# Input projection weights in 384-column half-row chunks, first convolution tap on ScalarE, channel transposes one tile later

## The chip, the core and the metric

The kernel runs on one core of one Trainium2 chip. The metric is device time in microseconds (us) of one execution; the time before is the median of three runs, 3180.53 us. TensorE (PE) loads weights (PEld) and multiplies; VectorE (DVE), ScalarE (ACT) and GpSimd (POOL) do the elementwise work; SyncE (SP) issues nearly all DMAs from one queue. Each engine runs its own instructions strictly in the order in which they were built.

## What is computed

One encoder layer over 2048 tokens of width 1024, all in float32. The part that the change touches is the first stage and the two branches that feed on it:

```python
h = rms_norm(x, g_mix[i])
proj = h @ w_in[i]                       # 1024 -> 2304 columns
q, k, v = proj[..., :512], proj[..., 512:640], proj[..., 640:768]
u = proj[..., 768:]                      # 1536 channels
ya = attention_group(q, k, v, ...)       # 8 query heads, 2 key heads
up = jnp.pad(u, ((0, 0), (1, 1), (0, 0)))
uc = conv_b + sum(up[:, j:j + L] * conv_w[j] for j in range(3))
v, x1, x2 = jnp.split(uc, 3, axis=-1)
z = x2 * long_conv(x1 * long_conv(v, H[0]), H[1])     # by FFT, filters from a small network
```

After it come the output projection, a mixture of experts, an embedding gate and a final norm, which the change leaves as they are.

## The kernel before

The projection is `stage_in` (line 105). It works on four quarters of 512 tokens. For each it loads four tiles of 128 tokens, normalises them, transposes them (L176) and splits them in a high and a low float32r part (`xh`, `xl`), since every float32 product is made of three float32r ones (`product`, L146 to 151). The weights are loaded (L134, `raw`) and split the same way in `split_w`: ACT rounds the high part (L139), and POOL (L89) or DVE (L143) subtracts it to get the low part.

Columns 0 to 767 (q, k, v) go through `tokens` (L182): three chunks of 256 columns, four token tiles each, with tokens as the stationary side, so each matmul streams 256 columns; ACT copies the result into a tile `stg`, which is stored to DRAM once per chunk (L190). Columns 768 on go through `channels` (L193): twelve tiles of 128 channels per quarter, channels on partitions and 512 tokens streamed. ACT copies the product into `U` (L205). The three-tap convolution is three DVE instructions: L210 multiplies the middle tap and adds the bias, L213 runs twice for the other two taps. PE then transposes the result back to tokens (L220), and ACT or DVE copies it into `stg` (L224, L226), which goes to DRAM (`uc_d`).

The whole runs beside a second stream. `interleave` (L92) builds two generators together, by the costs that they yield: the left one is `stage_in` and then attention, the right one is `stage_filter` (it generates the long filters: `gen`, a first FFT step L448 to L450, a second one L295), then `stage_hyena` (the long convolutions), then three tiles of the embedding projection (L1522 to L1540, `Ple`). The framework's scheduler then fixes the order on each engine. In `stage_hyena` every step keeps its result in one PSUM tile `ph`, of which there is only one: `step1` (L505) is the first FFT step, `mid` is a spread over frequencies (L295), a product on DVE (L529) and a gather (L308), and `back` (L545) is the inverse step. Between steps the data goes through DRAM. There are 32 of each. Attention runs in 16 units; their score matmuls are L806 and L809, the value ones L819, and `pa` (L741) are row maxima for later units. From the ninth unit on attention's PSUM banks include the two that hyena and `Ple` leave.

Of the kernel before, what the change touches and what calls it, by code (L numbers as in the profile page):

```python
# [8 lines left out]
F32 = mybir.dt.float32  # L9
F32R = mybir.dt.float32r  # L10
# [3 lines left out]
AF = mybir.ActivationFunctionType  # L14
ALU = mybir.AluOpType
# [3 lines left out]
P = 128  # L19
S = 2048  # L20
D = 1024
# [12 lines left out]
HY_LEAD = 0  # L34
HB = 3
FI_LATE = 1.5
GB = 8
GHB = 1
RB, WB = 13, 8
# [65 lines left out]
def stage_in(K, st, x, g_mix, w_in, conv_w, conv_b, qkv_d, uc_d, pa, attn):  # L105
# [16 lines left out]
    K.uc_done, K.banks_free = 0, False  # L122

    def consts():
        crow = pc.tile([48, P], F32, name="crow")
# [6 lines left out]
    def load_w(c0, n, pool, tag):  # L132
        raw = pool.tile([P, 8, n], F32, tag=tag, name="raw")
        nc.sync.dma_start(raw, w_in[:, c0:c0 + n].rearrange("(k p) n -> p k n", p=P))  # L134
        return raw

    def split_w(raw, n, pool, tags, on_pool, bufs=2):
        wh, wl = [pool.tile([P, 8, n], F32R, tag=tag, name=nm, bufs=bufs) for tag, nm in zip(tags, ("wh", "wl"))]
        nc.scalar.copy(wh, raw)  # L139
        if on_pool:  # L140
            K.lo_pool(wl, raw, wh)
        else:
            nc.vector.tensor_tensor(out=wl, in0=raw, in1=wh.bitcast(F32), op=ALU.subtract)  # L143
        return wh, wl

    def product(ps, left, right):  # L146
        for k in range(8):
            (lh, ll), (rh, rl) = left(k), right(k)
            nc.tensor.matmul(ps, lh, rh, start=(k == 0), stop=False)  # L149
            nc.tensor.matmul(ps, lh, rl, start=False, stop=False)  # L150
            nc.tensor.matmul(ps, ll, rh, start=False, stop=(k == 7))  # L151

    for h in range(NQ):
        last, first = h == NQ - 1, h > 0
        xh, xl = [[pa.tile([P, 4, HT], F32R, tag=f"{nm}{q}", name=nm) for q in range(2)] for nm in ("xh", "xl")]
        cols = [2, 0, 1] if last else [0, 1, 2]
        raws = []
        for t in range(HTT):
            r0 = h * HT + t * P
            xt = px.tile([P, D], F32, tag="xt", name="xt")  # L160
            nc.sync.dma_start(xt, x[r0:r0 + P])
            if r0 == 0:
                nc.sync.dma_start(gB, rows_bcast(g_mix))
            if t < 2:
                raws.append(load_w(cols[t] * 256, 256, praw, "raw"))
# [16 lines left out]
        def tokens(c, wh, wl):  # L182

            stg = pa.tile([P, HTT, 256], F32, tag="stg", name="stg", bufs=2)
# [8 lines left out]
        def channels(ct, stg, wh, wl):  # L193
# [10 lines left out]
            product(ps, lambda k: (wh(k), wl(k)), lambda k: xs(k, slice(None)))  # L204
            nc.scalar.copy(U[:, o0:o0 + HT], ps)  # L205
            if not last:
                nc.gpsimd.tensor_copy(bnd[:, ct], U[:, o0 + HT - 2:o0 + HT])
            n_out = HT + o0 - 1
            acc = pa.tile([P, HT + 4], F32, tag="acc", name="acc", bufs=2)
            nc.vector.tensor_scalar(out=acc[:, :n_out], in0=U[:, 1:1 + n_out], scalar1=wcol(1),  # L210
                                    scalar2=wcol(3), op0=ALU.mult, op1=ALU.add)
            for j in (0, 2):
                nc.vector.scalar_tensor_tensor(out=acc[:, :n_out], in0=U[:, j:j + n_out], scalar=wcol(j),  # L213
                                               in1=acc[:, :n_out], op0=ALU.mult, op1=ALU.add)
            if first:
                nc.gpsimd.tensor_copy(fix[:, h - 1, ct:ct + 1], acc[:, 0:1])
            pt = pst.tile([P, 512], F32, tag="pt", name="pt")
            for k in range(HTT):
                t0 = o0 - 1 + k * P
                nc.tensor.transpose(pt[:, k * P:(k + 1) * P], acc[:, t0:t0 + P], K.ident)  # L220
            dst = stg[:, :, ct % 2 * P:(ct % 2 + 1) * P]
            src = pt.rearrange("p (k c) -> p k c", k=HTT)
            if ct % 2:
                nc.scalar.copy(dst, src)  # L224
            else:
                nc.vector.tensor_copy(dst, src)  # L226

        for c in cols:
            raw = raws.pop(0) if raws else load_w(c * 256, 256, praw, "raw")
            if h == 0 and c == 0:  # L230
                consts()
            yield from tokens(c, *split_w(raw, 256, pw, ("wh", "wl"), not (c == 2 or (h == 0 and c < 2))))
        if last:
            while not K.filter_done:
                yield 0.05
            s_e.close()
            pb = attn.open(lambda tag: pst.tile([P, 512], F32, tag="pt", name=tag))
            ahead = attn.begin()
            raws = [load_w(768 + i * P, P, pb, "raw") for i in range(2)]
        for ct in range(12):  # L240
            part, cs = ct // 4, slice(ct // 2 % 2 * 256, (ct // 2 % 2 + 1) * 256)
            if last:
                raw = raws.pop(0)
                w4 = split_w(raw, P, pb, ("w", "w"), ct % 3 != 2, 4)
                if ct < 10:
                    raws.append(load_w(768 + (ct + 2) * P, P, pb, "raw"))
                wh, wl = [lambda k, w=w: w[:, k] for w in w4]
            else:
                if ct % 2 == 0:
                    raw = load_w(768 + ct * P, 256, praw, "raw")  # L250
                    w4 = split_w(raw, 256, pw, ("wh", "wl"), ct % 6 != 4)
                wh, wl = [lambda k, w=w: w[:, k, ct % 2 * P:(ct % 2 + 1) * P] for w in w4]
            if ct % 2 == 0:
                stg = pa.tile([P, HTT, 256], F32, tag="stg", name="stg", bufs=2)
            channels(ct, stg, wh, wl)
            yield 5.6
            if last:
                for _ in range(2):
                    if next(ahead, "end") != "end":
                        yield 0.44  # L260
# [1534 lines left out]
def block_kernel(tc, A, out):  # L1795
    K = Kit(tc)
    nc = tc.nc
# [9 lines left out]
    with ExitStack() as st:  # L1807
# [97 lines left out]
```

## Time and profile before

| | |
|---|---|
| median of three runs (lowest, highest) | 3180.53 us (3178.24, 3187.92) |
| the profiled execution, its span | 3189.39 us, 3187.4 us |
| PE busy | 2893.6 us, 91% |
| DVE, ACT, POOL busy | 66%, 43%, 37% |
| DMA, mean over the span | 197 GB/s |

Busy shares are means over stages with different limits; a stage is read by cutting it out of the span. "PEclk" is the TensorE clock that was granted in a stretch, as a share of 2.4 GHz; at 0.5 the engine runs at 1.2 GHz. A stretch loses time on PE in two ways: PE stands idle, or it works at the low clock.

### The profile page before, as it was taken

What the parts mean: (1) busy time and instruction counts of PE and PEld (TensorE: products, weight loads), DVE (VectorE), ACT (ScalarE), POOL (GpSimd) and SP (SyncE); (2) the same over time, 40 slices, a digit from 0 to 9 for tenths busy, and PEclk for the clock granted to TensorE, in tenths of its full rate; (3) what the DMA queues carried; (4) which work ended last, traced back from release to release, by engine and by line L of the source; (5) the groups of instructions that cost most, each with busy time, mean ns of one, the idle gap of its engine ahead of it and who ended that gap; (6) DMA issues with size and microseconds to landing.
All of it is one profiled execution on the core that took longest, in us unless ns stands there. A gap on an engine that the chain in (4) does not pass through costs nothing. (4 is left out here: it accounts for less than half of the span.)

```text
span 3187.4 us, 50724 instructions
## 1 busy us (share of the span) xinstructions
PE 2893.6 (91%) x19065; PEld 1942.2 (61%) x19065; DVE 2088.4 (66%) x2770; ACT 1357.0 (43%) x2040; POOL 1186.7 (37%) x1090
## 2 busy tenths in 40 slices
PE   7989898878899999759999999989999999998887
PEld 5767686655444453424444388866667777775766
DVE  5877767455687566527787644366667777775665
ACT  3343343432343334225444432245556666664332
POOL 1434544341365455228887543001111211221443
PEclk9999999888899999879999999989999999999998
DMA  6468797886656655651000254369789888997553
GB/s 195 145 205 254 229 276 216 229 267 199 200 176 180 190 163 167 179 170 32 18 18 10 65 167 142 140 216 320 249 275 351 293 300 285 308 333 245 178 179 112
DMA packets 471992, 627.48 MB, mean 197 GB/s; under 512 B 64597, under 2 KB 302984, under 8 KB 467262
## 3 DMA queue, kind: packets, MB, share of 16 engines
q1 hardware_dynamic: 451630, 568.73, 55.7%
q0 software_dynamic: 20112, 55.47, 5.4%
q8 instruction: 151, 2.47, 0.3%
q14 instruction: 99, 0.81, 0.1%
HBM read 462.45 MB, written 161.56 MB: 196 GB/s over the span
## 5 line engine op out<-in xcount | busy, mean ns | idle before, releaser
L1314 DVE TENSOR_TENSOR wl<-raw,wh 128x1024 fp32r<-128x1024 f32 x384 | 463.3, 1223 | 196.3 <-ACT wh L1309 187.5
L1309 ACT CAST wh<-raw 128x1024 fp32r<-128x1024 f32 x384 | 398.6, 1051 | 266.2 <-PE ps L1332 95.1
L829 POOL TENSOR_TENSOR sums<-e,sums 128x512 f32<-128x512 f32 x306 | 411.0, 1359 | 156.5 <-ACT e L810 152.1
L810 ACT ACTIVATE e<-ps 128x512 f32<-128x512 f32 x512 | 289.7, 597 | 345.7 <-PE ps L809 291.7
L743 DVE TENSOR_REDUCE mx<-pa 128x1 f32<-128x512 f32 x512 | 330.3, 682 | 111.7 <-PE pa L741 110.8
L819 PE MATMUL po<-e,v 128*64 128x512 f32 x1024 | 293.8, 627 | 3.5 <-ACT e L810 3.5
L1409 POOL DMA_DIRECT2D y_d<-ob x64 | 36.0, 565 | 590.0 <-DVE ob L1408 346.6
L1330 PE MATMUL ps<-wh,xt 128*128 128x512 f32 (+4 forms) x512 | 212.9, 416 | 6.8 <-ACT wh L1309 6.8
L1331 PE MATMUL ps<-wl,xt 128*128 128x512 f32 (+4 forms) x512 | 206.7, 404 | 5.9 <-DVE wl L1314 5.9
L1332 PE MATMUL ps<-wh,xt 128*128 128x512 f32 (+4 forms) x512 | 203.4, 397 | 0.0
L149 PE MATMUL ps<-xh,wh 128*128 128x512 f32 x384 | 155.4, 405 | 5.0 <-ACT U L205 5.0
L741 PE MATMUL pa<-kst,q 128*128 128x512 f32 x352 | 142.0, 454 | 18.3 <-DVE mx L743 12.9
L151 PE MATMUL ps<-xh,wl 128*128 128x512 f32 x384 | 154.4, 403 | 0.0
L150 PE MATMUL ps<-xl,wh 128*128 128x512 f32 x384 | 154.0, 401 | 0.0
L806 PE MATMUL ps<-q,kst 128*128 128x512 f32 x352 | 151.7, 431 | 0.0
L829 DVE TENSOR_TENSOR sums<-e,sums 128x512 f32<-128x512 f32 x110 | 123.9, 1133 | 35.4 <-ACT e L810 34.8
L809 PE MATMUL ps<-q,k 65*128 65x512 f32 x352 | 142.0, 403 | 4.8 <-DMA q<-mr 4.8
L89 POOL TENSOR_TENSOR wl<-raw,wh 128x2048 fp32r<-128x2048 f32 (+1 forms) x26 | 102.1, 3926 | 100.4 <-ACT wh L139 99.5
L741 PEld LDWEIGHTS pa<-kst,q 128*128 128x128 f32 x352 | 63.6, 193 | 121.9 <-DVE mx L743 66.8
L1336 PE MATMUL pr<-raw,xr 128*32 128x128 f32 (+1 forms) x2112 | 126.3, 303 | 1.6 <-DVE ob L1412 1.6
L1330 PEld LDWEIGHTS ps<-wh,xt 128*128 128x128 f32 (+4 forms) x512 | 95.6, 187 | 44.8 <-issue 14.3
L1279 POOL DMA_INDIRECT g<-h_d,idx x52 | 70.0, 1347 | 140.1 <-PE pt L1288 58.6
(379 smaller groups left out, 6761.0 us busy)
## 6 DMA issues: line engine op xcount, KB each, us to landing
raw<-in_w_gate_dram SPq DMA_DIRECT2D x128, 512.0 KB
raw<-in_w_up_dram SPq DMA_DIRECT2D x128, 512.0 KB
raw<-in_w_down_dram SPq DMA_DIRECT2D x128, 512.0 KB
h_f<-hs SPq DMA_DIRECT2D x256, 128.0 KB
ab<-h_f SPq DMA_DIRECT2D x32, 1024.0 KB
raw<-in_w_in_dram SPq DMA_DIRECT2D x30, 1024.0 KB
xt<-in_x_dram SPq DMA_DIRECT2D x32, 512.0 KB
dec<-in_c_decay_dram SPq DMA_DIRECT2D x64, 256.0 KB
```

The costliest lines, as they stand in the source:

```text
L149: nc.tensor.matmul(ps, lh, rh, start=(k == 0), stop=False)
L151: nc.tensor.matmul(ps, ll, rh, start=False, stop=(k == 7))
L741: nc.tensor.matmul(pa, qh[:, t * P:(t + 1) * P], self.kst[g][:, q * 512:(q + 1) * 512], start=True, stop=True)
L743: nc.vector.tensor_reduce(out=mx[:, t, q:q + 1], in_=pa, axis=AX.X, op=ALU.max)
L810: nc.scalar.activation(out=pe[:, i], in_=ps, func=AF.Exp, scale=0.125)
L819: mm = nc.tensor.matmul(po[H2[i]], v[:, kt, g * 64:(g + 1) * 64], pe[:, i], start=(kt == 0), stop=(kt == NT - 1), skip_group_check=True)
L829: acc[j][1].tensor_tensor(out=sums[j], in0=pe[:, i], in1=src, op=ALU.add)
L1309: nc.scalar.copy(hi, raw)
L1314: nc.vector.tensor_tensor(out=lo, in0=raw, in1=hi.bitcast(F32), op=ALU.subtract)
L1330: nc.tensor.matmul(ps[:m], xt[:, k, 0, :m], hv[:, j], start=(k == 0), stop=False)
L1331: nc.tensor.matmul(ps[:m], xt[:, k, 0, :m], lv[:, j], start=False, stop=False)
L1332: nc.tensor.matmul(ps[:m], xt[:, k, 1, :m], hv[:, j], start=False, stop=(k == 7))
```

## The change

- q, k and v are computed in two chunks of 384 columns instead of three of 256, and the convolution's channels in four chunks of 384 (three channel tiles) instead of six of 256. Each chunk's weights come in two pieces of 512 rows, each loaded and split by itself. There are four buffers for high pieces and three for low ones; before, there were two of each for whole chunks. The first four pieces and every third one are subtracted on DVE, the others on POOL.
- The result of `tokens` goes into a buffer shared with `U` and `acc` and is stored once per token tile.
- The middle tap with the bias moves from DVE to ACT.
- A channel tile's transposes are emitted after the next tile's product.
- `stage_hyena` is opened only when `stage_in` has given back its weight buffers (`K.room`).
- In the last quarter the channels' weights are loaded as before, in tiles of 128 columns.

```diff
+WC = 384
...
-    def split_w(raw, n, pool, tags, on_pool, bufs=2):
-        wh, wl = [pool.tile([P, 8, n], F32R, tag=tag, name=nm, bufs=bufs) for tag, nm in zip(tags, ("wh", "wl"))]
+    def split_w(raw, pool, tags, on_pool, bufs):
+        wh, wl = [pool.tile(list(raw.shape), F32R, tag=tag, name=nm, bufs=b)
+                  for tag, nm, b in zip(tags, ("wh", "wl"), bufs)]
...
+    def load_part(c, i):
+
+        return load_w(c * WC, WC, praw, slice(i * 512, (i + 1) * 512))
+
+    def chunk(c, raws=()):
+
+        parts = []
+        for i in range(2):
+            raw = raws[i] if raws else load_part(c, i)
+            n_piece[0] += 1
+            parts.append(split_w(raw, pw, ("wh", "wl"), n_piece[0] > 4 and n_piece[0] % 3 != 0, (4, 3)))
+        return lambda k, cols: [w[:, k % 4, cols] for w in parts[k // 4]]
...
-                product(ps[:, :256], lambda k: xs(k, slice(t * P, (t + 1) * P)), lambda k: (wh[:, k], wl[:, k]))
-                nc.scalar.copy(stg[:, t], ps[:, :256])
-                yield 2.6
-            nc.sync.dma_start(qkv_d[h * HT:(h + 1) * HT, c * 256:(c + 1) * 256]
-                              .rearrange("(t p) n -> p t n", p=P), stg)
+                product(ps[:, :WC], lambda k: xs(k, slice(t * P, (t + 1) * P)), lambda k: w(k, slice(0, WC)))
+                so = pa.tile([P, HT + 4], F32, tag=("U", "acc")[t % 2], name="so", bufs=2)[:, :WC]
+                nc.scalar.copy(so, ps[:, :WC])
+                nc.sync.dma_start(qkv_d[h * HT + t * P:h * HT + (t + 1) * P, c * WC:(c + 1) * WC], so)
+                yield 4.3
...
-            nc.vector.tensor_scalar(out=acc[:, :n_out], in0=U[:, 1:1 + n_out], scalar1=wcol(1),
-                                    scalar2=wcol(3), op0=ALU.mult, op1=ALU.add)
+            nc.scalar.activation(out=acc[:, :n_out], in_=U[:, 1:1 + n_out], func=AF.Identity, scale=wcol(1),
+                                 bias=wcol(3))
...
+                made = (ct, *channels(ct, w))
+                yield 5.6
+                if late is not None:
+                    yield late
+                late = made
+                if last and ct % 4 == 3:
+                    yield late
+                    late = None
...
             K.filter_done = True
+            while not K.room:
+                yield 0.05
             with ExitStack() as s1:
                 for c in stage_hyena(K, s1, A["c_wa"], uc_d, h_f, s_z, t_z, yh_d):
```

How the order of instructions changes is shown at three places.

**The taps, on DVE, in the first quarter's channels.** Before, the low-part subtraction of a chunk, the first tap and the two others stood on DVE:

```order
L143 TENSOR_TENSOR wl<-raw,wh 128x2048
L210 TENSOR_SCALAR acc<-U,cw 128x512
L402 TENSOR_TENSOR g<-pd,dec 128x512
L213 SCALAR_TENSOR_TENSOR acc<-U,cw,acc 128x512
L402 TENSOR_TENSOR g<-pd,dec 128x512
L403 TENSOR_REDUCE part<-g 128x128
L213 SCALAR_TENSOR_TENSOR acc<-U,cw,acc 128x512
```

Now the first tap is an ACTIVATE on ACT, behind the copy of the product, with a weight piece's rounding between the tiles:

```order
L141 CAST wh<-raw 128x1536
L221 COPY U<-ps 128x512
L226 ACTIVATE acc<-U,cw 128x512
L221 COPY U<-ps 128x512
L226 ACTIVATE acc<-U,cw 128x512
L243 COPY stg<-pt 128x4x128
```

DVE keeps the two other taps; ACT has one instruction more per channel tile.

**The end of the filters and the first hyena steps, on PE, in the last quarter** (`pd<-zt` is the filters' last step, `ph<-z` hyena's first). Before, hyena's first steps stood ahead of the last five channel tiles:

```order
L741 MATMUL pa<-kst_6461,q_6686 128x512
L505 MATMUL ph<-z,w1d 128x512 x2
L741 MATMUL pa<-kst_6461,q_6686 128x512
L274 MATMUL fp<-ident,fix 4x128 x3
L505 MATMUL ph<-z,w1d 128x512 x4
L149 MATMUL ps<-xh,wh 128x512
```

Now the filters' last steps stand there, with one channel tile behind them:

```order
L333 MATMUL pd<-zt,w_506 64x128 x16
L239 MATMUL pt<-ident,acc 128x128 x8
L312 MATMUL fp<-ident,fix 4x128 x3
L779 MATMUL pa<-kst_6134,q_6356 128x512 x7
L543 MATMUL ph<-z,w1d 128x512 x2
L779 MATMUL pa<-kst_6134,q_6356 128x512
L543 MATMUL ph<-z,w1d 128x512 x2
L166 MATMUL ps<-xh,wh 128x512
```

Ahead of attention's first value matmul stood 8 `step1`, 8 spreads and 7 gathers before; now 7 `step1` and none of the others.

**The end of hyena, on PE, between the first matmuls of attention's eighth unit and the rest of it.** Before, this stretch held 5 spreads, 6 gathers and 8 `back`, and ended so:

```order
L741 MATMUL pa<-kst_7903,q_12580 128x512 x2
L308 MATMUL ph<-ab,wa 64x128 x32
L295 MATMUL ph<-zt,w_553 64x128 x16
L308 MATMUL ph<-ab,wa 64x128 x32
L295 MATMUL ph<-zt,w_553 64x128 x16
L308 MATMUL ph<-ab,wa 64x128 x32
L545 MATMUL ph<-bt,wb 64x512 x16
L1522 MATMUL pt<-ident,pr 128x128 x2
```

Now it holds 7 pairs of `back` and `step1`, 8 spreads, 8 gathers and 8 `back`; one passage of it is:

```order
L583 MATMUL ph<-bt,wb 64x512 x2
L543 MATMUL ph<-z,w1d 128x512 x2
L583 MATMUL ph<-bt,wb 64x512 x2
L543 MATMUL ph<-z,w1d 128x512 x2
L333 MATMUL ph<-zt,w_506 64x128 x16
L346 MATMUL ph<-ab,wa 64x128 x32
```

In both, 19 `pa` matmuls and `Ple` are all that stands there besides. Behind this stretch PE's order is the same as before but for a few places where neighbours are swapped.

## Rows read from the trace of the kernel before

**Rows 1.** Stretches: length; busy PE, PEld, DVE, ACT, POOL; clock, DMA share, GB/s.

```profile
0.00:46.00 46.00, 22.99 (x121) 17.74 (x122) 24.40 (x45) 17.20 (x27) 3.46 (x14) 0.89 0.85 255
46.00:700.00 654.00, 579.40 (x4740) 467.74 (x4740) 465.65 (x533) 253.70 (x394) 281.09 (x269) 0.95 0.73 219
700.00:834.00 134.00, 97.11 (x950) 67.39 (x948) 66.11 (x90) 34.06 (x54) 17.08 (x40) 0.82 0.70 220
834.00:1298.00 464.00, 444.00 (x3261) 214.19 (x3258) 323.91 (x453) 188.28 (x312) 248.88 (x201) 0.98 0.60 179
1298.00:1413.00 115.00, 63.02 (x644) 37.20 (x642) 35.97 (x50) 14.89 (x21) 1.64 (x1) 0.67 0.60 172
1413.00:1820.00 407.00, 392.88 (x1499) 178.93 (x1501) 311.23 (x426) 192.47 (x343) 318.04 (x229) 0.99 0.12 33
```

**Rows 2.** Waits of PE up to 834 us: total, times, longest (us).

```profile
PE pt L220 <- DVE acc L213: 26.8, 17, 5.7
PE ph L505 <- DMA z<-uc_d: 10.7, 2, 8.0
PE ps L372 <- DVE sa L362: 10.5, 1, 10.5
```

**Rows 3.** Timeline of PE: starts of matmuls of 256 and of 512 columns.

```profile
605.07 0.28 PE L151 MATMUL ps<-wh,xl 128*128 128x256 f32 x1
...
605.90 0.28 PE L149 MATMUL ps<-wh,xh 128*128 128x256 f32 x1
...
1297.92 0.39 PE L809 MATMUL ps<-ql,k 65*128 65x512 f32 x1
...
1298.38 0.40 PE L809 MATMUL ps<-ql,k 65*128 65x512 f32 x1
```

**Rows 4.** The channel tile's first tap and copy up to 900 us: busy, mean ns.

```profile
L210 DVE TENSOR_SCALAR acc<-U,cw 128x513 f32<-128x513 f32 x36 | 50.5, 1402 | 32.1 <-ACT U L205 31.4 <-PE pt L220 0.8
L205 ACT COPY U<-ps 128x512 f32<-128x512 f32 x48 | 28.1, 586 | 41.4 <-PE ps L151 20.1 <-DVE acc L213 9.5 <-issue 9.1
L210 DVE TENSOR_SCALAR acc<-U,cw 128x512 f32<-128x512 f32 x12 | 18.5, 1539 | 4.7 <-ACT U L205 4.7
```

**Rows 5.** Line L210 over the span: shortest, median, longest (ns).

```profile
L210 DVE TENSOR_SCALAR acc<-U,cw x48: 531/546/4445, 85.5 to 794.6; 128x513 f32<-128x513 f32 x36, 128x512 f32<-128x512 f32 x12
```

**Rows 6.** Timeline: POOL's split of a chunk and a DVE instruction beside it, twice.

```profile
174.12 4.51 POOL L89 TENSOR_TENSOR wl<-raw,wh 128x2048 fp32r<-128x2048 f32 x1 [4.65 <-ACT wh L139]
...
174.56 4.36 DVE L210 TENSOR_SCALAR acc<-U,cw 128x512 f32<-128x512 f32 x1 [0.21 <-ACT U L205]
...
610.88 4.62 POOL L89 TENSOR_TENSOR wl<-raw,wh 128x2048 fp32r<-128x2048 f32 x1 [1.84 <-ACT wh L139]
...
611.35 4.69 DVE L81 TENSOR_TENSOR gl<-g,gh 128x512 fp32r<-128x512 f32 x1 [7.01 <-ACT gh L80]
```

**Rows 7.** Timeline of PE beside attention: two step1 three apart, a spread.

```profile
1239.89 1.13 PE L505 MATMUL ph<-z,w1d 64*128 64x512 f32 x4
...
1267.31 1.13 PE L505 MATMUL ph<-z,w1d 64*128 64x512 f32 x4
...
1282.00 1.10 PE L295 MATMUL ph<-zt,w 64*64 64x128 f32 x32
```

**Rows 8.** Timeline of PE at hyena's end: gathers, then back.

```profile
1300.71 1.98 PE L308 MATMUL ph<-ab,wa 64*64 64x128 f32 x64 [0.49 <-PE pa L841]
...
1330.16 1.98 PE L308 MATMUL ph<-ab,wa 64*64 64x128 f32 x64 [2.08 <-issue]
...
1336.92 3.95 PE L308 MATMUL ph<-ab,wa 64*64 64x128 f32 x64 [2.52 <-issue]
...
1346.53 3.51 PE L308 MATMUL ph<-ab,wa 64*64 64x128 f32 x64 [2.52 <-issue]
1351.21 1.08 PE L545 MATMUL ph<-bt,wb 128*64 128x512 f32 x4 [1.17 <-ACT sg L533]
...
1384.43 1.97 PE L545 MATMUL ph<-bt,wb 128*64 128x512 f32 x4 [2.88 <-DMA bt<-t_z]
```

More of the change, by code (lines that the diff above doesn't have):

```diff
@@ L121, in stage_in @@
     gB = pc.tile([P, D], F32, name="gB")
-    K.uc_done, K.banks_free = 0, False
+    K.uc_done, K.banks_free, K.room = 0, False, False
     def consts():
@@ L130, in consts, with load_w @@
         nc.scalar.copy(cw, cps[:, :48])
-    def load_w(c0, n, pool, tag):
-        raw = pool.tile([P, 8, n], F32, tag=tag, name="raw")
-        nc.sync.dma_start(raw, w_in[:, c0:c0 + n].rearrange("(k p) n -> p k n", p=P))
-        return raw
-    def split_w(raw, n, pool, tags, on_pool, bufs=2):
-        wh, wl = [pool.tile([P, 8, n], F32R, tag=tag, name=nm, bufs=bufs) for tag, nm in zip(tags, ("wh", "wl"))]
+    def load_w(c0, n, pool, rows=slice(0, D)):
+        raw = pool.tile([P, (rows.stop - rows.start) // P, n], F32, tag="raw", name="raw")
+        nc.sync.dma_start(raw, w_in[rows, c0:c0 + n].rearrange("(k p) n -> p k n", p=P))
+        return raw
+    def split_w(raw, pool, tags, on_pool, bufs):
+        wh, wl = [pool.tile(list(raw.shape), F32R, tag=tag, name=nm, bufs=b)
+                  for tag, nm, b in zip(tags, ("wh", "wl"), bufs)]
         nc.scalar.copy(wh, raw)
@@ L155, in stage_in @@
         xh, xl = [[pa.tile([P, 4, HT], F32R, tag=f"{nm}{q}", name=nm) for q in range(2)] for nm in ("xh", "xl")]
-        cols = [2, 0, 1] if last else [0, 1, 2]
+        cols = [1, 0] if last else [0, 1]
         raws = []
@@ L164, in stage_in @@
             if t < 2:
[L165 removed]
+                raws.append(load_part(cols[0], t))
             xn = px.tile([P, D], F32, tag="xn", name="xn", bufs=1)
@@ L180, in stage_in, with tokens, channels @@
         xs = lambda k, ts: (xh[k // 4][:, k % 4, ts], xl[k // 4][:, k % 4, ts])
[L182 to L184 removed]
+        def tokens(c, w):
             for t in range(HTT):
                 ps = psm.tile([P, 512], F32, tag="pm", name="ps")
[L187 to L193 removed]
+                product(ps[:, :WC], lambda k: xs(k, slice(t * P, (t + 1) * P)), lambda k: w(k, slice(0, WC)))
[3 more added lines that the diff above has]
+                yield 4.3
+        def channels(ct, w):
             wcol = lambda j: cw[:, j * 12 + ct:j * 12 + ct + 1]
@@ L203, in channels @@
             ps = psm.tile([P, 512], F32, tag="pm", name="ps")
-            product(ps, lambda k: (wh(k), wl(k)), lambda k: xs(k, slice(None)))
+            product(ps, w, lambda k: xs(k, slice(None)))
             nc.scalar.copy(U[:, o0:o0 + HT], ps)
@@ L216, in channels, with token_major @@
                 nc.gpsimd.tensor_copy(fix[:, h - 1, ct:ct + 1], acc[:, 0:1])
+            return acc, o0 - 1
+        def token_major(ct, acc, o0, stg):
             pt = pst.tile([P, 512], F32, tag="pt", name="pt")
             for k in range(HTT):
-                t0 = o0 - 1 + k * P
+                t0 = o0 + k * P
                 nc.tensor.transpose(pt[:, k * P:(k + 1) * P], acc[:, t0:t0 + P], K.ident)
@@ L228, in stage_in @@
         for c in cols:
-            raw = raws.pop(0) if raws else load_w(c * 256, 256, praw, "raw")
+            w = chunk(c, raws)
+            raws = ()
             if h == 0 and c == 0:
                 consts()
-            yield from tokens(c, *split_w(raw, 256, pw, ("wh", "wl"), not (c == 2 or (h == 0 and c < 2))))
+            yield from tokens(c, w)
         if last:
@@ L236, in stage_in @@
             s_e.close()
+            K.room = True
             pb = attn.open(lambda tag: pst.tile([P, 512], F32, tag="pt", name=tag))
             ahead = attn.begin()
-            raws = [load_w(768 + i * P, P, pb, "raw") for i in range(2)]
-        for ct in range(12):
-            part, cs = ct // 4, slice(ct // 2 % 2 * 256, (ct // 2 % 2 + 1) * 256)
[L242 to L252, printed above, removed]
+            raws = [load_w(768 + i * P, P, pb) for i in range(2)]
@@ new lines, in convolved @@
+        def convolved():
+            late = None
+            for ct in range(12):
+                if last:
+                    w2 = split_w(raws.pop(0), pb, ("w", "w"), ct % 3 != 2, (4, 4))
+                    if ct < 10:
+                        raws.append(load_w(768 + (ct + 2) * P, P, pb))
+                    w = lambda k: [a[:, k] for a in w2]
+                else:
+                    if ct % 3 == 0:
+                        w3 = chunk(2 + ct // 3)
+                    w = lambda k: w3(k, slice(ct % 3 * P, (ct % 3 + 1) * P))
+                made = (ct, *channels(ct, w))
[5 more added lines that the diff above has]
+                    yield late
+                    late = None
+            if late is not None:
+                yield late
@@ L253, in stage_in @@
+        for step in convolved():
+            if isinstance(step, float):
+                yield step
+                if last:
+                    for _ in range(2):
+                        if next(ahead, "end") != "end":
+                            yield 0.44
+                continue
+            ct, acc, o0 = step
+            part, cs = ct // 4, slice(ct // 2 % 2 * 256, (ct // 2 % 2 + 1) * 256)
             if ct % 2 == 0:
                 stg = pa.tile([P, HTT, 256], F32, tag="stg", name="stg", bufs=2)
-            channels(ct, stg, wh, wl)
@@ L256, in stage_in @@
[L256 to L260, printed above, removed]
+            token_major(ct, acc, o0, stg)
             if ct % 2 == 0:
```

1 line of the change is left out of this document (added).

## The prediction, before the changed kernel was run

> **What bounds the kernel now.** The page's chain of waits covers under a tenth of the span, at its end, so the stage that the change touches is read from the stretches instead [rows 1]. Up to 834 us (attention's first value matmul) the projection runs beside the filters; from there to 1298 attention runs beside hyena; to 1413 hyena's last steps stand on PE almost alone; to 1820 attention runs by itself. Beside hyena PE is busy 444 of 464 us, in attention by itself 392.9 of 407: there only less PE work would save time. Before 834 PE is busy 579.4 + 23.0 + 97.1 = 699.5 us and idle 134.5, and the low clock takes more: 0.11 of 23.0, 0.05 of 579.4 and 0.18 of 97.1, together 49 us. Between 1298 and 1413 PE is busy 63 us at a clock of 0.67, and DMA moves only 172 GB/s: neither is full, a chain of dependent steps is. So there are two places to look at: the 183 us lost before 834, and the length of hyena's tail.
>
> Who makes PE wait before 834? The largest entry is the transposes of a channel tile, which wait for DVE's last tap, 26.8 us in 17 waits [rows 2]. Why is DVE late? The first tap takes 546 ns in the median and 4.4 us at the longest [rows 5]; its mean is 1.4 to 1.5 us [rows 4]. The timeline shows one long case: the tap starts 0.4 us after a POOL split of a weight chunk and ends when that split ends [rows 6].
>
> **The change, part by part.**
> *Fewer, longer matmuls.* Seven steps of 256 columns take 605.90 − 605.07 = 0.83 us, 0.119 each; two of 512 take 0.46, 0.23 each [rows 3]. For 384 the value between is 0.174. 768 × 0.174 − 1152 × 0.119 = −3 us (bounds: −5 if 384 go in proportion to 512 columns, 0 if to 256). It is PE work, so it counts whole.
>
> *Copies, splits, loads, stores.* ACT copies the same columns in 32 instructions instead of 48. Splits keep their elements: 24 pieces of three quarters the size on POOL are the 18 chunks of before, 16 on DVE the 12. Loads become 40 for 30 in the first part, stores of q, k, v 32 for 12, so SP issues 30 more; what stands behind them on its queue is the filters' traffic, and PE's list has no large wait for that traffic, only for hyena's `z` [rows 2]. I put all of these at nothing; the cover is the buffers, and if it goes, each chunk's second low piece, with a third buffer instead of a second pair, is the first to be late: the split starts when the last product has used half its rows, and POOL needs three quarters of 4.6 us, 3.4 [rows 6], against 24 matmuls of 0.174, 4.2 us. With 20 chunks the bounds are 0 and some 10 us.
>
> *The first tap on ACT.* DVE loses 50.5 + 18.5 = 69 us [rows 4], of which 48 × 0.546 = 26 are its own work and 43 are waiting for POOL. ACT gains 48 × about 0.59 (its copy of the same tile [rows 4]) = 28 us and is busy 253.7 of 654 us [rows 1], so that hides. What inherits the wait? The two taps that stay on DVE read two SBUF operands each, and the second timeline pair shows such an instruction, `gl`, taking 4.69 us beside a split of 4.62 [rows 6]. So part of the 43 us passes to the second tap; but it starts about 0.6 us later, and splits are 3.4 us instead of 4.6, so a meeting costs at most about 2.8 instead of 3.9. The Trainium skill, SBUF — State Buffer, section Who interferes with whom, says that a DVE instruction in a two-port mode, or with two SBUF inputs while GpSimd reads SBUF, blocks for all of the GpSimd instruction. The trace agrees, with 4.36 and 4.69.
>
> *The transposes later.* One channel tile is 24 × 0.23 = 5.5 us of PE work. PE's built order had some other work between a product and its transposes already, but unevenly; now about a tile's worth or more stands there everywhere but at the end of a quarter. A meeting of 2.8 us hides in that, one at a quarter's end doesn't. I take 22 of the 26.8 us as gone.
>
> *What that gives before 834.* From 46 to 700 us, 74.6 idle and 29 of clock: 22 of idle and, since the stretches with gaps are those at the low clock [rows 1], 12 of clock: 34. At the start PE waits for DVE's sine steps, 10.5 us [rows 2]; ahead of that wait stand three token tiles, now longer by 72 × (0.174 − 0.119) = 4 us: 4. From 700 to 834, where 36.9 + 17.5 are lost, `z` keeps its 10.7, and 15 spreads and gathers with a single PSUM tile go elsewhere: 12. Together 50, bounds 25 (half) and 75.
>
> *Hyena moved back.* Ahead of the first value matmul PE loses one `step1` (1.13), 8 spreads (1.10) and 7 gathers (1.98): −24 us [rows 7, 8]. Beside attention the work hardly changes: 6 `step1` and 7 `back` (1.08) fewer, 5 spreads and 5 gathers more, +1. The rest lands in the tail, where PE has nothing to do beside it. The tail was 115 us [rows 1]: mids at 45.8 / 5 = 9.2 us (1300.71 to 1346.53), the quickest 6.8 [rows 8]; 8 `back` and then the embedding tiles from 1351 to 1413, 62 us, which stay. Now come 7 pairs of `back` and `step1`. A pair's chain is 1.08, then DVE, then 1.13, then ACT's copy, at least 4.2 us by these rows with 1 us each for DVE and ACT; beside attention three pairs took 27.4 us, 9.1 each [rows 7]. I take 5.3, nearer to the chain, since attention isn't there. Then 3 us until the first spread's data has come back from DRAM, 8 mids at 8.0, and the 62: 37 + 3 + 64 + 62 = 166, so +51. The bounds: 7 × 4.2 + 8 × 6.8 + 62 = 146, +31, and 7 × 9.1 + 3 + 8 × 9.2 + 62 = 202, +87.
>
> **The sum:** −3 − 50 − 24 + 1 + 51 = −25 us. The profiled execution took 3189.4 us, so 3164; the median of the runs lies 8.9 below that execution, which gives 3155.
>
> **The rivals.**
> *The tail runs at the chain's best.* Nothing but hyena is on the engines there, and loads of the next steps can run ahead (DMA moved 172 GB/s there, and 255 at the start [rows 1]). Then the tail grows by 31 and the rest stays: −45, 3135. Against it: the clock falls in the tail, gathers there take 3.5 to 3.95 instead of 1.98 [rows 8].
>
> *The tail is bound by DMA, and the kernel is slower.* A pair moves 1.25 MB (`bt` 0.5, `gt` 0.25, the spectrum 0.5), a mid 2 MB, a `back` without `step1` 1 MB, by the tiles' shapes: 7 × 1.25 + 8 × 2 + 8 × 1 = 33 MB. At the 172 GB/s of the tail before that is 191 us, with 26 for the embedding tiles 217 instead of 115: +102, and the sum is +26, 3206. It decides from +76 on, where it eats the other terms. For it: nearly every `back` in the tail waited for a transfer [rows 8]. Against it: other stretches move 219 to 255 GB/s [rows 1].
>
> *The wait only changes hands.* Splits and taps keep meeting, the second tap waits as long as the first did, PE stalls at the transposes as before, and of the 50 us only half comes, from the start, the moved steps and a part of the clock: the sum is 0, 3180. For it: `gl` [rows 6]. Against it: the later transposes. By the rule of the Trainium skill's SBUF — State Buffer alone (section Who interferes with whom), with a tap blocked for a whole split each time they meet, this would be the case.
>
> **How the numbers follow.** The sum as forecast 0.47, the quick tail 0.18, the slow tail 0.15, the wait that changes hands 0.20. A measurement here tells about 0.3% (9.5 us) from no change. Of the forecast nearly all is faster by that, of the quick tail all; the changed hands give half to the same, a little to faster and slower; the slow tail mostly slower. Faster 0.64, same 0.20, slower 0.16. The range goes from the quick tail with more idle time gained (3116) to half of the slow tail's price above none (3196).
>
> **What would show it.** Right: the first tap at about 0.6 us on ACT and no DVE instruction of the taps above 3.5 us; the wait of transposes for taps under 8 us; attention's first value matmul near 755 us (834 less 77); the stretch up to attention's eighth unit unchanged in length; the tail, from the last attention matmul ahead of it to the next, near 166 us; after it all as before. Wrong: a first value matmul later than 800 us (the losses didn't fall), a tail under 145 or over 190, waits of PE for low weight pieces of more than 10 us, or a second stretch that grows by more than 15 us, since I hold it to be PE work.

## The result, and the profile after

The changed kernel takes 3202.77 us (median of 6 runs, 3192.09 to 3206.57) against 3184.1 for the kernel before beside it (6 runs): ratio 1.0051, 95% interval 1.0038 to 1.0064. It is slower by half a per cent; 3155 was forecast. The profiled execution took 3202.06 us, its span is 3200.3, against 3187.4: +12.9.

The stretches of the changed kernel, cut at the same events as before, answer to [rows 1] (length; busy PE, PEld, DVE, ACT, POOL; clock, DMA share, GB/s). 787.5 us is attention's first value matmul, 1256.4 the end of its seventh unit, 1433.6 the first attention matmul behind hyena's tail:

```profile
0.00:46.00 46.00, 29.07 (x130) 22.79 (x131) 25.25 (x46) 20.08 (x30) 3.33 (x10) 0.89 0.82 262
46.00:715.00 669.00, 580.76 (x4270) 462.99 (x4269) 437.29 (x510) 280.81 (x429) 273.70 (x290) 0.93 0.68 204
715.00:787.50 72.50, 57.65 (x314) 34.49 (x313) 26.94 (x41) 29.76 (x47) 8.28 (x22) 0.81 0.87 268
787.50:1256.40 468.90, 447.78 (x3705) 224.78 (x3704) 341.04 (x471) 189.57 (x317) 257.13 (x208) 0.98 0.62 183
1256.40:1433.60 177.20, 98.58 (x912) 55.08 (x911) 43.41 (x57) 22.40 (x27) 1.64 (x1) 0.61 0.64 188
1433.60:1835.00 401.40, 392.69 (x1505) 178.74 (x1507) 314.06 (x425) 192.69 (x343) 317.89 (x229) 1.00 0.12 34
```

In the kernel before the same events lie at 833.7, 1300.2, 1413.0 and the span's end. So:

| stretch | before | after | difference | forecast |
|---|---|---|---|---|
| up to the first value matmul | 833.7 | 787.5 | -46.2 | -77 |
| to the end of the seventh unit | 466.5 | 468.9 | +2.4 | +1 |
| hyena's tail | 112.7 | 177.2 | +64.5 | +51 |
| the rest | 1774.4 | 1766.7 | -7.7 | 0 |

Up to the first value matmul PE is busy 667.5 us (699.5 before) and idle 120.0 (134.5). Of the 32 us of work that went, 30 are hyena's steps (42.1 us of PE's time before, 12.0 now), which only come later; of the idle time 14.5 us went. What PE waits for up to 834 us is another list than [rows 2] (total, times, longest):

```profile
PE ps L486 <- ACT gh L81: 25.5, 6, 11.6
PE pd L433 <- ACT hs L501: 23.0, 5, 13.6
PE ps L166 <- ACT xh L81: 8.4, 4, 7.1
...
PE pt L239 <- DVE acc L229: 4.1, 3, 3.0
```

The 26.8 us of waiting for the last tap are down to 4.1 (L239 in the changed kernel). In their place PE waits for copies and roundings of ACT; of the first three lines the third belongs to the projection, the others to the filters. The wait list of ACT has the next link (first the kernel before, then the changed one), and that of SP's queue up to 740 us the one behind it:

```profile
ACT wh L139 <- DMA raw<-in_w_in_dram: 7.8, 3, 5.7
```

```profile
ACT wh L141 <- DMA raw<-in_w_in_dram: 124.0, 20, 20.5
```

```profile
SPq L135 <- DVE wl L145: 26.0, 9, 7.1
SPq L135 <- POOL wl L90: 23.7, 11, 5.7
```

ACT waits 124.0 us for weight pieces (7.8 before). A piece's load, behind others on SP's queue, first waits for a low part to be split off so that one of the two raw buffers comes free. SP waits for splits in the kernel before too (17.5 and 14.4 us at its load, L134), but its two raw buffers hold whole chunks, so that each load has a longer lead; run 12 below shows that one raw buffer more takes ACT's wait away. One case, with the lines of the engines that take part, start and length in us:

```profile
331.32 7.33 SPq L507 DMA_DIRECT2D h_f<-hs  x8
...
339.22 0.39 SPq L135 DMA_DIRECT2D raw<-in_w_in_dram  x1
...
346.10 1.47 ACT L141 CAST wh<-raw 128x1536 fp32r<-128x1536 f32 x1 [11.55 <-DMA raw<-in_w_in_dram]
347.47 1.01 ACT L501 COPY hs<-pd 128x1024 f32<-128x1024 f32 x1
348.38 0.62 ACT L81 CAST gh<-g 128x512 fp32r<-128x512 f32 x1
...
348.53 0.70 PE L433 MATMUL pd<-w,h 64*64 64x128 f32 x8 [13.64 <-ACT hs L501]
```

Eight stores of the filters stand ahead of the load on SP. The rounding of that piece stands ahead of the filters' copy `hs` on ACT, and PE can't write `pd` until `hs` is copied. PE is idle for 13.64 us. That looks like the whole answer. The experiments show that it isn't.

### The profile page after: what moved, and what is told of

Read it like the earlier page. It is cut to its first block, busy times and chain, and to the rows that moved or that the text cites. A ratio compares the mean times of both kernels' runs of the same rounds, so it can differ in the third digit from the quotient of the medians.

```text
span 3200.3 us, 50042 instructions
## 1 busy us (share of the span) xinstructions
PE 2898.3 (91%) x18681; PEld 1937.8 (61%) x18681; DVE 2047.4 (64%) x2726; ACT 1391.1 (43%) x2082; POOL 1175.9 (37%) x1096
## 4 chain that ended last, share of the span: by engine, by line
PE 58%; DMA 11%; DVE 8%; issue 4%; ACT 2%; POOL 2%; SPq 1%; DVEq 0%; POOLq 0%; ACTq 0%
PE po L857 7%; PE pa L779 4%; PE ps L1368 4%; PE ps L1369 4%; PE ps L1370 4%; PE ps L844 4%; PE ps L847 3%; PE pr L1374 3%; PE ph L346 2%; PE ps L1434 2%; PE ps L1436 2%; PE ps L1435 2%; PE pr L1441 2%; PE ps L1007 2%; PE ps L1008 2%
## 5 line engine op out<-in xcount | busy, mean ns | idle before, releaser
L779 PE MATMUL pa<-kst,q 128*128 128x512 f32 x352 | 143.0, 453 | 26.8 <-DVE mx L781 19.2
L141 ACT CAST wh<-raw 128x1536 fp32r<-128x1536 f32 (+1 forms) x52 | 71.6, 1377 | 153.0 <-DMA raw<-in_w_in_dram 124.0
L867 POOL TENSOR_TENSOR sums<-e 128x512 f32<-128x512 f32 x31 | 42.6, 1379 | 245.1 <-ACT e L848 203.7
L229 DVE SCALAR_TENSOR_TENSOR acc<-U,cw,acc 128x513 f32<-128x513 f32 (+1 forms) x96 | 88.1, 920 | 60.8 <-ACT acc L226 44.5
```

The source lines that it names most:

```text
L779: nc.tensor.matmul(pa, qh[:, t * P:(t + 1) * P], self.kst[g][:, q * 512:(q + 1) * 512], start=True, stop=True)
L867: acc[j][1].tensor_tensor(out=sums[j], in0=pe[:, i], in1=src, op=ALU.add)
```

## The experiments

Each ratio is against the kernel before, run on the same chip, where its median was 3188.5 to 3190.7 us for runs 1 to 16, so the ratios are to be compared and not the medians. "Pieces" is ACT's wait for raw weights up to 800 us; "filters' end" is the start of the last matmul of the filters' spreads, "first value" that of attention's first value matmul; "tail" is hyena's tail, cut at the same events as above.

| run | median us | ratio (95%) | pieces | filters' end | first value | tail |
|---|---|---|---|---|---|---|
| before | 3184.1 | 1 | 7.8 | 681.1 | 833.7 | 112.7 |
| changed | 3202.8 | 1.0051 (1.0038 to 1.0064) | 124.0 | 737.2 | 787.5 | 177.2 |
| 1 tap alone | 3177.5 | 0.9962 (0.9947 to 0.9977) | 9.0 | 699.5 | 800.2 | 138.5 |
| 2 late transposes alone | 3156.1 | 0.9895 (0.9860 to 0.9930) | 8.4 | 682.6 | 786.0 | 134.4 |
| 3 both | 3172.7 | 0.9942 (0.9922 to 0.9962) | 6.4 | 668.8 | 794.0 | 137.7 |
| 4 all 256 wide, raw 4, low 4 | 3150.3 | 0.9879 (0.9845 to 0.9914) | 16.1 | 659.1 | 775.6 | 138.2 |
| 5 tokens 256 wide | 3215.5 | 1.0095 (1.0066 to 1.0123) | 153.6 | 718.8 | 830.6 | 133.8 |
| 6 channels 256 wide | 3216.2 | 1.0094 (1.0066 to 1.0123) | 146.6 | 731.2 | 782.3 | 168.1 |
| 7 as 4, raw 2 | 3166.7 | 0.9938 (0.9919 to 0.9956) | 49.2 | 690.7 | 796.3 | 137.8 |
| 8 as 4, tap on DVE | 3155.5 | 0.9900 (0.9874 to 0.9926) | 13.1 | 667.1 | 783.1 | 134.1 |
| 9 before, raw 1 | 3182.8 | 0.9990 (0.9978 to 1.0001) | 45.2 | 694.1 | 831.8 | 110.8 |
| 10 as 4, low 3 | 3173.3 | 0.9950 (0.9933 to 0.9967) | 13.9 | 680.9 | 791.4 | 141.2 |
| 11 as 4, raw 2, low 3 | 3222.9 | 1.0101 (1.0072 to 1.0129) | 190.4 | 735.6 | 843.6 | 139.2 |
| 12 changed, raw 3, high 3 | 3201.2 | 1.0044 (1.0026 to 1.0062) | 10.8 | 724.3 | 768.1 | 181.3 |
| 13 as 12, filters' PSUM 2 | 3158.2 | 0.9899 (0.9873 to 0.9926) | 10.1 | 659.6 | 776.0 | 135.4 |
| 14 changed, filters' PSUM 2 | 3158.1 | 0.9892 (0.9858 to 0.9925) | 107.5 | 667.2 | 782.6 | 135.7 |
| 15 as 12, tokens 2 x 192 | 3180.6 | 0.9955 (0.9939 to 0.9971) | 6.7 | 665.9 | 808.1 | 111.7 |
| 16 as 4, filters' PSUM 2 | 3165.0 | 0.9927 (0.9901 to 0.9953) | 7.5 | 640.4 | 783.5 | 135.7 |

**The parts without the chunks (1 to 3), and all of it 256 wide (4).** Run 1 puts the changed kernel's `scalar.activation` for the first tap into the kernel before, run 2 its `token_major` and `convolved` around the old chunks, run 3 both. Run 4:

```diff
-WC = 384
+WC = 256
-    praw, pw = pool("in_raw", 2), pool("in_w", 2)
+    praw, pw = pool("in_raw", 4), pool("in_w", 2)
-... (4, 3)))
+... (4, 4)))
```

> The kernel before with the first tap on ScalarE and nothing else changed. Theory A (the change lost by its weight chunks: with two buffers of half a chunk the loads come late, ScalarE stands waiting for them, and the filters slip, so that hyena's tail grows): taken alone the tap is harmless; PE's wait for the last tap falls from 26.8 to about 15 us, other waits of PE for ScalarE rise by less than 5 us, hyena's tail stays near 115 us, time 3170 to 3182 us. Theory B (ScalarE itself is too full with the taps): PE's waits for ScalarE before attention's first value matmul rise by 20 us or more, time 3184 to 3200. Theory C (waits only change hands): PE's idle time before 834 us stays within 6 us of 134.5, time 3180 to 3188.

> The kernel before with each channel tile's transposes one channel tile later and nothing else changed. If the 26.8 us in which PE waits for the last tap are a loss that counts (the prediction's step), that wait falls under 8 us and the time to 3160 to 3170 us. If the wait only covers others that come later anyway (theory C), the wait falls as much but PE's other waits rise by as much, time 3180 to 3188 us.

> The kernel before with the tap on ScalarE and the later transposes, but its own weight chunks (256 columns, whole rows, two buffers of a whole chunk). Theory A: ScalarE's wait for weight pieces stays under 15 us (7.8 before, 124 in the changed kernel), PE's idle time before the first value matmul falls by 15 us or more, tail near 115 us, time 3150 to 3172 us, better than both kernels. Theory B: PE's waits for ScalarE's casts and copies rise by 20 us or more as in the changed kernel, time 3184 or more. Theory C: 3178 to 3188.

> The changed kernel with chunks of 256 columns, still by halves of the rows, with four raw pieces (two chunks, as before) and four low pieces; all else as changed. Theory A: ScalarE's wait for weight pieces falls from 124 to under 20 us, the tail from about 180 to about 115 us, time 3150 to 3172 us. If the halves or the tap are to blame instead of the width and the buffers, PE's waits for ScalarE stay near the 57 us of the changed kernel and the time stays above 3185 us.

The later transposes by themselves bring 1.05%, 34 us, more than the wait that they took from 26.8 to 8.3 us. They were quicker than the 3160 to 3170 us that were expected. The tap alone brings 0.4% (that wait falls to 17.1), and added to the transposes it brings nothing more (0.9942 against 0.9895; the intervals overlap, and the wait is 16.6 us against 8.3). Where these expectations have the tail near 115 us, it came at 138. Run 4 has every part of the change but the width, the buffer counts and the cost yielded to `interleave` that go with it, and is 1.2% faster. So the loss sits in the width or the buffers. ACT's load alone (theory B) is out: run 4 has the tap on ACT too.

**Width (5, 6), raw pieces (7), the tap (8).** Runs 5 and 6 give the token products and the channel chunks a width each (`WT, WCH = 256, 384` and `384, 256`), two raw and three low pieces as in the changed kernel. Run 7 is run 4 with `pool("in_raw", 2)`, run 8 run 4 with the `vector.tensor_scalar` of before.

> The changed kernel with only the token products (q, k, v) in chunks of 256 columns; the channel chunks stay 384 wide, with two raw pieces and three low pieces. Theory W (the wide token tiles did it: the filters' steps stand on TensorE's list between token and channel tiles, 16 tiles fewer are 16 places fewer, so the filters end later and hyena's tail grows): the filters' last spread comes near 680 us instead of 737, the tail is near 115 us and the time 3145 to 3165 us. Theory A (two raw pieces make ScalarE wait for weights and the filters with it): 20 pieces of the channel chunks still come late, the time stays at 3180 us or more, ScalarE's wait for pieces above 50 us.

> The reverse: the changed kernel with only the channel chunks 256 wide, the token products stay 384 wide. Theory W: as the changed kernel, filters' last spread after 725 us, tail 170 us or more, time 3185 to 3205 us. Theory A: the pieces of most chunks are now two thirds as large and come sooner, ScalarE's wait for them halves or better and the time falls to 3160 to 3180 us.

> All chunks 256 wide as in the fourth run (3150.3 us), with two raw pieces instead of four, so that one chunk can be loaded ahead instead of two. Theory A: ScalarE's wait for pieces rises to 60 us or more, PE's waits for ScalarE by 15 us or more, and the time to 3170 us or more. Theory W: ScalarE may wait, but the time stays within 10 us of 3150, since ScalarE has slack.

> The fourth run (256 wide by halves, later transposes) with the first tap back on VectorE. In whole-row chunks the tap on ScalarE cost 16 us on top of the later transposes (3172.7 against 3156.1). If that is ScalarE's load, the tap on VectorE is the quicker here too: 3135 to 3147 us. If by-halves pieces leave POOL's splits short enough either way, no difference: 3147 to 3155. If the tap on ScalarE is what the halves need (VectorE waits for POOL again), 3156 to 3170 us.

In run 5 half of theory W came true: with narrow token tiles the tail is 43 us shorter than in the changed kernel (133.8 against 177.2). But ACT waits 153.6 us for pieces, as theory A had it, the first value matmul comes 43 us later (830.6 against 787.5), and the kernel is as slow as ever. Theory A fails in run 6, where the smaller pieces were waited for longer and the time, 3216.2, is above both forecasts. Run 7 falls between its two theories and puts a price on two raw pieces: 33 us more waiting, 16 us of time. Run 8 can't be told from run 4: with these shorter splits it doesn't show which engine has the tap.

**The buffers one by one (9 to 12).** Each is a change of pool counts alone: 9 `pool("in_raw", 1)` in the kernel before, 10 and 11 `(4, 3)` in runs 4 and 7, 12 `pool("in_raw", 3)` with `(3, 3)` in the changed kernel.

> The kernel before with one raw weight buffer of a whole chunk instead of two: as many bytes loaded ahead as in the changed kernel, a little more, but its own widths, tap and transposes. Theory A: ScalarE's wait for raw weights rises from 7.8 to 60 us or more, and the time by 15 us or more over the kernel before (ratio 1.005 or above). Theory L (not the loads, but the third low piece holds the splits up in the changed kernel): ScalarE waits somewhat, the ratio stays within 0.3% of 1.

> The fourth run (256 wide, four raw pieces, 3150.3 us) with three low pieces instead of four. Theory A: ScalarE's wait for raw pieces stays under 30 us, time 3145 to 3165 us. Theory L: the splits wait for the low buffer, the raw pieces come free late, wait 60 us or more, time 3175 us or more.

> All chunks 256 wide, two raw pieces and three low pieces, the buffer counts of the changed kernel. Theory A: as the run with two raw pieces and four low ones (49 us of waiting, 3166.7 us), within 10 us. Theory L: wait 100 us or more, time 3190 or more. Both together (a raw piece comes free only when its low piece has found a place): wait 70 to 120 us, 3175 to 3200.

> The changed kernel at its own 384 columns with three raw pieces and three high pieces instead of two and four, the same bytes of SBUF. Theory A: ScalarE's wait for raw pieces falls from 124 to under 80 us and the time to 3170 to 3192 us, although the built order of the filters' steps is as late as in the changed kernel. If the built order is what counts, or the high pieces are then what is missing (casts wait for PE), the time stays at 3198 us or above.

At 256 columns the two counts cost more together than their sum: fewer raw pieces cost 0.6%, fewer low ones 0.7%, both 2.2%. Run 10 lies between the times of its two theories. In it the low part is what is late (POOL waits 30.1 us for PE before L90), but four raw pieces keep ACT fed; in run 11 ACT waits 190.4 us, as theory L has it and more than both together were said to cost. That a raw piece comes free there only when its low part has found a place fits this, but was not shown by itself. Run 9 shows that a short lead alone does little: 45.2 us of waiting, no loss.

Run 12 is the surprise. It takes the wait away at the change's own width, and nothing is gained. First the line of the filters' spreads in the changed kernel (shortest, median, longest ns; first and last start us), then ACT's wait and the same line in run 12:

```profile
L333 PE MATMUL pd<-zt,w x1024: 269/269/473, 229.5 to 737.2; 64*64 64x128 f32 x171
```

```profile
ACT wh L141 <- DMA raw<-in_w_in_dram: 10.8, 3, 6.8
```

```profile
L333 PE MATMUL pd<-zt,w x1024: 269/269/473, 220.6 to 724.3; 64*64 64x128 f32 x171
```

The first value matmul comes at 768.1, 65.6 us earlier than before, 13 us from the 755 that was forecast. But the filters end at 724.3, 43 us later than before, hyena starts behind them, and its tail runs from 1244.7 to 1426.0: 181.3 us. What was gained ahead was given back there. The rival named beforehand, that high pieces are then missing, plays no part that shows: run 13 has as few, and run 14 with four is no quicker.

**One PSUM buffer for the filters (13 to 16).** The filters have 32 spreads of 16 matmuls each in the built order, 512 in all (the trace counts 1024, two for each); the numbers here and in the expectations are of these matmuls. In the kernel before, 208 of the filters' generating matmuls and 64 of the 512 of the spreads stand ahead of the second quarter's channels in the built order; in the changed kernel 144 and none. Ahead of the last quarter's channels stand 448 of the 512 before, 336 in the changed kernel and in runs 6 and 12, and 448 in all others. The filters' FFT steps share one PSUM buffer. Runs 13, 14 and 16 move one to them; the built order then has 448 again:

```diff
-    pst, psm = pool("in_pt", 2, s_ps, space=PSUM), pool("in_pm", 3, s_ps, space=PSUM)
+    pst, psm = pool("in_pt", 2, s_ps, space=PSUM), pool("in_pm", 2, s_ps, space=PSUM)
...
-    pc, psm, psd = pool("fi_c", 1), pool("fi_p", 1, space=PSUM), pool("fi_d", 1, space=PSUM)
+    pc, psm, psd = pool("fi_c", 1), pool("fi_p", 2, space=PSUM), pool("fi_d", 1, space=PSUM)
```

Run 15 keeps run 12's buffers and makes each token tile of two products of 192 columns, which also brings the 448 back.

> The twelfth run (384 columns, three raw and three high pieces, 3201.2 us, ScalarE's wait for pieces 10.8 us, the filters' last spread at 724 us) with one PSUM buffer taken from the projection's three and given to the filters' one. In the built order 448 of the filters' 512 spreads then stand ahead of the last quarter's channel tiles, as in the kernel before; 336 in the changed kernel. Theory F (what sets the time is when the filters end, since hyena starts there and the end of the stage follows hyena's end): last spread at 670 to 700 us, tail near 120 us, time 3150 to 3180 us. Rival (the wide tiles cost something else, on PE or in attention): the filters end earlier but the time stays at 3195 us or above.

> The changed kernel with that PSUM buffer moved and its own buffers (two raw, four high, three low pieces). Theory F with the loads: ScalarE still waits 100 us or more for pieces, the filters stand behind it and end at 710 to 740 us though the built order has them early: 3190 to 3215 us. If the order alone decides, 3150 to 3180 us.

> The twelfth run with each token tile's product as two of 192 columns instead of one of 384: the chunks, loads, splits and PSUM buffers stay, PE gets 768 more matmuls (some 10 to 30 us more work by the pitch of 256 columns as upper bound), and the built order has 448 spreads ahead of the last quarter's channel tiles. Theory F: the filters end before 705 us and the time falls below 3195 us in spite of the added work. Rival: the added work shows, 3205 to 3230 us.

> The quickest kernel so far (fourth run: 256 wide by halves, four raw, four high, four low pieces, 3150.3 us, last spread at 659 us) with the PSUM buffer moved to the filters. Theory F: the filters' waits for their one buffer go, the last spread comes 10 us or more earlier and the time falls by 5 to 20 us, to 3130 to 3145 us. If two buffers are too few for the projection, PE waits for copies instead: 3150 to 3175 us.

Run 13 against run 12, and run 14 against the changed kernel, are one buffer moved each, and 43 and 45 us. In the profiled executions they are 45 and 46 us, and nearly all of that lies in the tail: it is 45.9 and 41.5 us shorter, while the first value matmul comes 7.9 us later and 4.9 us earlier. These are the tails of run 12 and of run 14, in the columns of [rows 1]:

```profile
1244.70:1426.00 181.30, 99.75 (x916) 53.73 (x915) 44.27 (x58) 22.46 (x28) 1.64 (x1) 0.62 0.66 194
```

```profile
1246.60:1382.30 135.70, 74.16 (x860) 46.47 (x859) 39.50 (x51) 15.40 (x21) 1.64 (x1) 0.64 0.66 189
```

In run 14 (ACT's wait; the filters' spreads; PE's waits for ACT):

```profile
ACT wh L141 <- DMA raw<-in_w_in_dram: 107.5, 22, 9.4
```

```profile
L333 PE MATMUL pd<-zt,w x1024: 269/269/473, 199.1 to 667.2; 64*64 64x128 f32 x171
```

```profile
PE ps L486 <- ACT gh L81: 18.7, 7, 4.9
PE pd L433 <- ACT hs L501: 2.3, 1, 2.3
```

ACT waits nearly as long as in the changed kernel, yet the filters end 70 us sooner and the time is that of run 13. The first branch of its expectation was wrong, the second came true: here the late loads cost nothing that shows. That is no rule: in runs 7 and 11 the filters stand as early in the built order, and the first value matmul comes 21 and 52 us later than in runs 4 and 10, where the loads are in time. What spares run 14, whose filters have two PSUM buffers and not one, was not tried. Run 15 pays 1536 x 0.112 - 768 x 0.176 = 37 us of added PE work (the steps of 192 columns are shown at the end) and is still 20 us faster than run 12. It brings the early order back without moving a buffer, and its tail is 69.6 us shorter than run 12's. That wide tiles cost time in some other way is not borne out: runs 13 and 14 keep them and are quick. Run 16 missed: the filters end at 640.4, 19 us sooner than in run 4, and the time is no shorter (0.9927 against 0.9879; the intervals overlap). Its tail, 135.7, is about that of run 4, and the first value matmul came at 783.5 instead of 775.6. The rival named for it, PE waiting for the projection's copies, is 3.0 us there, so what holds that matmul up stays open.

Over all eighteen kernels the tail goes with the built order. With 448 spread matmuls ahead, hyena starts 81 us or more before the first value matmul, the tail is 111 to 141 us, and the span ends 2340 to 2381 us behind that matmul. With 336 (changed kernel, 6, 12) hyena starts 29 to 37 us before it, the tail is 168 to 181 us, and the span ends 2413 to 2430 us behind it. The spread of some 40 us in the first group is only in part the tail's; the rest is not explained. No kernel with chunks of 384 columns is clearly quicker than run 2, the later transposes alone (0.9895; runs 13 and 14 have 0.9899 and 0.9892): what the wider chunks and the tap bring of themselves shows in no run.

## Why the prediction was wrong, point by point

- **Fewer, longer matmuls: right.** Steps of 384 columns take 0.176 each, 0.174 was said; eight of them lie between these two starts:

```profile
564.00 0.34 PE L166 MATMUL ps<-wh,xh 128*128 128x384 f32 x1
...
565.41 0.33 PE L168 MATMUL ps<-wh,xl 128*128 128x384 f32 x1
```

- **The first tap: right in kind, short in size.** On ACT it takes 818 ns in the median, not 590: 39.3 us in all. The longest DVE tap takes 3.77 us; 3.5 was the bound named. The two taps that stay cost 88.2 us instead of 78.4, so 10 of the 43 us were inherited. The Trainium skill, SBUF — State Buffer, section Who interferes with whom, has the port pair that the two engines share held for a whole instruction by the one that issued first. The trace agrees: the longest tap starts 0.78 us into a POOL split of 3.98 us and ends about 0.6 us behind it. The row of the tap on ACT, then the two others on DVE, then that meeting:

```profile
L226 ACT ACTIVATE acc<-U,cw x48: 805/818/846, 78.0 to 773.2; 128x513 f32<-128x513 f32 x36, 128x512 f32<-128x512 f32 x12
```

```profile
L229 DVE SCALAR_TENSOR_TENSOR acc<-U,cw,acc x96: 650/754/3765, 79.2 to 774.9; 128x513 f32<-128x513 f32 x72, 128x512 f32<-128x512 f32 x24
```

```profile
154.82 3.98 POOL L90 TENSOR_TENSOR wl<-raw,wh 128x1536 fp32r<-128x1536 f32 x1
...
155.60 3.77 DVE L229 SCALAR_TENSOR_TENSOR acc<-U,cw,acc 128x512 f32<-128x512 f32 x1
```

- **The transposes later: right.** The wait fell by 22.7 us; 22 was said. Run 2 shows that it counts. That waits only change hands, a rival, is half true: they did not pass to the transposes again, but PE's waits for ACT's copies rose.
- **"I put all of these at nothing; the cover is the buffers": this step failed.** It looked for PE waiting for low pieces, which PE hardly does (2.0 us). The shortage shows two engines away, as 124 us of ACT waiting for a load, and reaches PE through the filters' copies behind that wait: 52 us against 12 before. That ate the 34 us said for the stretch from 46 to 700, where idle time rose from 74.6 to 88.2 us (to 715 in the changed kernel). Of the 77 us forecast before the first value matmul 46 came, and 30 of them are hyena's moved steps; of the 50 us of lost time that were to come back, the idle time gave 14.5 and the clock nothing (0.93 before and 0.92 now, up to that matmul). Run 12 gives the failed step its size: with the wait taken away the first value matmul comes 19.4 us earlier, but the kernel is no quicker, so this step alone is not the loss. The bound of 0 to 10 us for the third low buffer was too tight: at 256 columns it cost 23 us with four raw pieces, 56 with two.
- **The tail: the mechanism right, the size short.** The pairs of `back` and `step1` follow at 4.3 to 6.0 us, one at 11.0 (5.3 was taken, 4.2 and 9.1 the ends), most mids at 9.4 (8.0); answering to [rows 8], from the timeline of the changed kernel:

```profile
1286.92 1.97 PE L583 MATMUL ph<-bt,wb 128*64 128x512 f32 x4 [1.16 <-ACT sg L545]
...
1292.92 1.97 PE L583 MATMUL ph<-bt,wb 128*64 128x512 f32 x4 [1.16 <-ACT sg L545]
...
1304.44 3.69 PE L346 MATMUL ph<-ab,wa 64*64 64x128 f32 x64 [2.56 <-DVE ab L567]
...
1313.85 3.69 PE L346 MATMUL ph<-ab,wa 64*64 64x128 f32 x64 [2.56 <-DVE ab L567]
```

  From the first of the seven `back` to the first spread it took 45.5 us (40 was said), the eight mids 73.0 (64), what follows 60.7 (62). These gathers ran at the low clock, 0.5 (3.69 us; 1.98 at the full one in [rows 8]), as they had in the old tail's second half; over the whole tail the granted clock was 0.61. The old tail's mean of 9.2 was the better figure for a mid: the new mean is 9.1. The rival of a tail bound by DMA had 217 us at 172 GB/s; it took 177.2 at 188. One reading for that rival was too strong: of the eight `back` of the old tail five waited for a transfer, not nearly every one.
- **What was missing altogether** is the link between the stretches. The sum took time before the first value matmul as won whatever else happens, and the tail as a price of its own. Run 12 shows that they are tied: with the loads cured the first of them reached -65.6 us and the tail took 68.6. The prediction read from the built order that hyena was moved back, but took that as given and not as the thing to mend: runs 13 to 15 show that the late place of the filters' steps is what makes the tail long, and that it can be mended. With them early again the change is worth -1.1% (run 14). That this is close to the -0.8% that was forecast is luck: it comes as 51 us ahead of the first value matmul and 23 us more tail, where 77 and 51 were said.
- **The signs named.** None of the four signs of being wrong came: the first value matmul lay under 800 us, the tail under 190, the waits for low pieces were 2.0 us, and the second stretch grew by 2.4. A miss of 31 us ahead of the first value matmul and of 13 in the tail fitted between the signs of right and of wrong.

That hyena waits for the weight buffers (`K.room`) does not by itself hold it back: runs 4 and 13 have that wait too, and hyena starts 94 and 93 us before the first value matmul there (35 in the changed kernel). The wait alone, in the kernel before, was not tried. Why the built order holds the filters back when the token tiles are wide is argued, not shown: they fill places between the projection's steps, and with one PSUM buffer each of their steps waits for the copy of the one before.

## What to carry to other kernels

Before an idle gap is counted as a gain, ask which chain starts when: time won ahead of a stretch is lost in its tail if the work that feeds the tail has been moved back. A shortage of buffers need not show as a wait of the engine that uses them; follow the load back to the split that frees its buffer, and look at what stands behind the waiting instruction on its engine. At 384 columns a second PSUM buffer for the filters, taken from a stream that has three, was worth 43 to 45 us, where their steps stood late without it; at 256 columns, where they stood early already, it brought nothing (run 16). Whether it helps the kernel before was not tried.

## What the runs showed of the hardware that was not expected

An ACTIVATE with a scale and a bias for each partition on 128 x 513 elements takes ACT 818 ns, where a copy of 128 x 512 from PSUM takes 587. Matmuls of 192 columns hardly come closer together than those of 256: ten steps of 192 in run 15 take 1.12 us, 0.112 each, where 256 columns take 0.119 [rows 3] and 384 take 0.176. Its timeline:

```profile
571.60 0.27 PE L166 MATMUL ps<-wh,xh 128*128 128x192 f32 x1
...
572.72 0.27 PE L167 MATMUL ps<-wl,xh 128*128 128x192 f32 x1
```
